# Gate projections of a decoder layer: hi and lo halves in one moving operand, a weight sum formed by accumulating DMAs, scratch reads moved a block ahead

## Chip, cores and metric

One core of a Trainium2 chip runs one launch. The metric is the time of the launch in microseconds, the median of several executions; the kernel before takes 1435.92 us.

## What is computed

A single layer: RMS norm with adaLN modulation, one input projection, a convolution branch and a differential-attention branch, both gated, merged by sigmoid gates of the input, and an output projection. The part that the change touches is the projection onto three of its column ranges, cz, m_conv ("mc") and m_attn ("ma"):

```python
h = rms_norm(x, g_pre[l]) * (1.0 + scale[:, None, :]) + shift[:, None, :]
p = h @ w_in[l]                                    # h: 512 x 2048
cv, cg, cz, q, k, v, az, m_conv, m_attn = jnp.split(p, offsets, axis=-1)
...
u = jax.nn.silu(u) * jax.nn.silu(cz)               # cz: 1024 columns
o = o.reshape(B, S, ATTN_WIDTH) * jax.nn.silu(az)
merged = jax.nn.sigmoid(m_conv) * y_conv + jax.nn.sigmoid(m_attn) * y_attn   # 2048 columns each
```

## The kernel before

Float32 operands are kept as sums of two float32r parts, hi and lo. `split` (L143) makes them: ScalarE copies hi (L145), VectorE subtracts for lo (L146). A product is then three matmuls, hi·hi, hi·lo and lo·hi, issued by `mm3` (L165, matmul on L167). h stands as 16 tiles of 128 rows (k = 0 to 15), each a pair tile `[128, 2, 512]` with hi and lo beside each other.

Stages in order: input norm and the conv projection, values, queries, keys and heads, then the az projection (L643 to L658) and then the gates (L803 to L824). The gates are 20 blocks of 256 output columns: 4 of cz, 8 of ma, 8 of mc. In a block `gemm_blocks` (L681) multiplies a 2 x 2 arrangement of weight blocks (a11, a21 in raw tile r1; a12, a22 in r2; each 128 x 8 x 128) with a 2 x 2 arrangement of h by Strassen's scheme in Winograd's form: seven products of 256 moving columns and eight k in place of eight products. It needs four sums of weights (s1 = a21 + a22, s2 = s1 + a11, s3 = a11 + a21, s4 = s2 + a12; L705, L706, L715, L724, on VectorE, 1024 elements wide) and sums of h (T1 to T4). Products go to three PSUM banks z, xx and y, in the order z, x, y, x, z, x, y; between them VectorE combines the results in 256-wide instructions (L711, L714, L718, L723, L727).

```python
def prod(ps, w, b, first):
    hi, lo = w
    for k in range(KH):
        mm3(ps[:, :H2], (hi[:, k, :], lo[:, k, :]), b[k], first and k == 0, k == KH - 1, not first, ordered)
    pump(rate[0])
```

The sums of h are made during the az stage by `block_sums` (L614), a generator whose steps `pump` (L478) inserts after each weight split there (three steps at a time); it splits T2 and T3 together (`t23`, 512 wide) and T4 for two k at a time. In the gates `pump` inserts steps of the convolution statistics (`conv_stats`, L747; `pmean` is its first matmul, behind the first product). `paced` and `ordered` keep the marked instructions in the order of the program; the rest is placed by a scheduler, and each engine runs its queue in order.

Temporaries come from the pool `mp`, which the stage before the gates holds under `front`; `front.close()` (L667) frees it and the gates open a pool of their own in the same memory. Weights come by `wraw` (L153, 1 MB each, three buffers, SP's queue) and are split by `wsplit` (L158) into hi and lo with three buffers each. Results are written to DRAM scratch by `spill` and read again by `fetch` (L433, L437), also on SP's queue. In ma, o and az are fetched after the block's products, multiplied (L820), split and spilled. GpSimd's queue has no DMA.

## Time and profile before

| | |
|---|---|
| runs | 1434.68, 1435.92, 1436.1 us; median 1435.92 |
| profiled execution | 1436.9 us, of it 1435.1 us span from the first to the last instruction |
| TensorE (PE) busy | 97% of the span |
| VectorE (DVE), ScalarE (ACT) busy | 75%, 36% |
| GpSimd (POOL) busy | 1.8 us |
| DMA queues | one of data, 237.31 MB |
| mean granted TensorE clock | 0.995 |

PE is matmuls, PEld weight loads, which overlap them; SPq is SyncE's queue of DMA issues. The start of an instruction and its duration are given, and durations of neighbours overlap in a pipeline, so the pace of an engine is the difference of starts. A wait is put down to what ended it. Stretches are given from the span's start.

### The profile page before, as it was taken

The page shows a single profiled execution, that of the slowest core. Times are in us where ns is not written, and L with a number is a line of the kernel's source. Part 1 is how long each engine was busy: PE and PEld are TensorE (multiplying, and loading weights), DVE is VectorE, ACT ScalarE, POOL GpSimd, SP SyncE. Part 2 cuts the span into 40 slices and gives each one's busy share as a digit, 9 for nine tenths or more (in the row PEclk, how much of TensorE's full clock was granted, in tenths as well). Part 3 has the DMA queues.
Part 4 walks back from the last instruction along what each step waited for, and adds up shares of the span by engine and source line. Part 5 has one row for each costly group of instructions (what it writes and reads, how often), then busy time and mean ns, then how long its engine had stood idle before and what let it go on. Part 6 is the DMA issues. An engine that isn't in the chain of part 4 may idle for free.

```text
span 1435.1 us, 20362 instructions
## 1 busy us (share of the span) xinstructions
PE 1397.3 (97%) x7999; PEld 1189.5 (83%) x7999; DVE 1080.9 (75%) x1750; ACT 522.1 (36%) x839; POOL 1.8 (0%) x8
## 2 busy tenths in 40 slices
PE   5899999999999999999999999999999999999997
PEld 4676787887777867788999999999998888888885
DVE  6997976988888887588988878777767676526645
...
GB/s 301 288 280 304 237 123 92 125 121 59 117 67 96 103 67 84 86 111 142 224 128 192 198 170 174 172 140 121 134 233 350 280 243 181 88 107 231 190 147 147
DMA packets 178338, 238.62 MB, mean 166 GB/s; under 512 B 8689, under 2 KB 119618, under 8 KB 177346
## 3 DMA queue, kind: packets, MB, share of 16 engines
q1 hardware_dynamic: 178242, 237.31, 49.9%
...
q14 instruction: 33, 0.27, 0.1%
HBM read 210.02 MB, written 27.26 MB: 165 GB/s over the span
## 4 chain that ended last, share of the span: by engine, by line
PE 90%; DVE 5%; DMA 2%; ACT 1%; issue 1%; SPq 0%; DVEq 0%; ACTq 0%
PE pw L167 12%; PE pc L167 11%; PE py_ya L167 6%; PE py_yc L167 6%; PE pv L167 6%; PE pg_az L167 5%; PE pg_q L167 5%; PE pg_k L167 5%; PE x_ma L167 5%; PE x_mc L167 4%; PE z_ma L167 3%; PE y_ma L167 3%; PE y_mc L167 3%; PE z_mc L167 3%; PE x_cz L167 2%; PE y_cz L167 2%
## 5 line engine op out<-in xcount | busy, mean ns | idle before, releaser
L500 DVE SCALAR_TENSOR_TENSOR cacc<-u,cw,cacc 128x511 f32<-128x511 f32 (+14 forms) x240 | 164.4, 728 | 0.0
L167 PE MATMUL pc<-hp,wh_c 128*128 128x512 f32 x512 | 159.9, 397 | 3.0 <-DVE part L369 1.2
L167 PE MATMUL pw<-wh_o,mgs 128*128 128x512 f32 x448 | 140.6, 393 | 0.0
L167 PEld LDWEIGHTS pc<-hp,wh_c 128*128 128x128 f32 x512 | 95.6, 190 | 29.0 <-issue 2.7
L167 PE MATMUL pc<-hp,wl_c 128*128 128x512 f32 x256 | 99.0, 396 | 2.1 <-DVE wl_c L146 2.1
L167 PEld LDWEIGHTS pw<-wh_o,mgs 128*128 128x128 f32 x448 | 84.1, 188 | 18.9 <-ACT fsq L932 0.7
L167 PE MATMUL pw<-wl_o,mgs 128*128 128x512 f32 x224 | 87.2, 389 | 0.0
L369 DVE TENSOR_TENSOR part<-pc,part 128x512 f32<-128x512 f32 x96 | 64.7, 687 | 25.3 <-PE pc L167 25.0
L167 PE MATMUL pv<-wh_v,hp 128*128 128x512 f32 x256 | 82.8, 397 | 0.9 <-DVE part L369 0.9
L167 PE MATMUL pg_q<-hp,wh_q 128*128 128x512 f32 x256 | 82.7, 398 | 0.0
L167 PE MATMUL pg_az<-hp,wh_az 128*128 128x512 f32 x256 | 81.5, 395 | 0.0
L167 PE MATMUL pg_k<-hp,wh_k 128*128 128x512 f32 x256 | 80.1, 392 | 0.0
L167 PE MATMUL py_ya<-ya,wh_ya 128*128 128x512 f32 x256 | 78.7, 389 | 0.0
L146 DVE TENSOR_TENSOR wl_o<-wr_o,wh_o 128x1024 fp32r<-128x1024 f32 x28 | 34.2, 1222 | 52.7 <-ACT wh_o L145 52.7
L145 ACT CAST wh_c<-wr_c 128x1024 fp32r<-128x1024 f32 (+1 forms) x36 | 34.2, 955 | 104.0 <-DMA wr_c<-in_w_in_dram 54.9
L889 DVE SCALAR_TENSOR_TENSOR accg<-adag,cact,accg 128x512 f32<-128x512 f32 x60 | 45.1, 751 | 32.2 <-DMA adag<-in_w_ada_dram 31.1
L145 ACT CAST wh_o<-wr_o 128x1024 fp32r<-128x1024 f32 x28 | 29.5, 1052 | 104.5 <-PE pw L167 93.0
L167 PEld LDWEIGHTS pc<-hp,wl_c 128*128 128x128 f32 x256 | 48.5, 190 | 14.1 <-DVE wl_c L146 3.3
L167 PEld LDWEIGHTS pv<-wh_v,hp 128*128 128x128 f32 x256 | 47.8, 188 | 14.3 <-issue 4.5
L167 PEld LDWEIGHTS pg_az<-hp,wh_az 128*128 128x128 f32 x256 | 47.7, 188 | 12.0 <-issue 2.7
L167 PEld LDWEIGHTS pg_q<-hp,wh_q 128*128 128x128 f32 x256 | 47.2, 188 | 12.4 <-issue 2.8
L167 PEld LDWEIGHTS py_ya<-ya,wh_ya 128*128 128x128 f32 x256 | 48.0, 188 | 9.9
...
## 6 DMA issues: line engine op xcount, KB each, us to landing
ada<-in_w_ada_dram SPq DMA_DIRECT2D x128, 256.0 KB, 5.4
wr_ma<-in_w_in_dram SPq DMA_DIRECT2D x16, 1024.0 KB
wr_mc<-in_w_in_dram SPq DMA_DIRECT2D x16, 1024.0 KB, 5.2
...
wr_o<-in_w_o_dram SPq DMA_DIRECT2D x16, 1024.0 KB, 5.1
...
wr_v<-in_w_in_dram SPq DMA_DIRECT2D x8, 1024.0 KB, 5.1
wr_q<-in_w_in_dram SPq DMA_DIRECT2D x8, 1024.0 KB, 5.0
```

The source lines that it names most:

```text
L145: nc.scalar.copy(hi, src)
L146: i = nc.vector.tensor_tensor(lo, src, hi.bitcast(F32), op=ALU.subtract)
L167: mm = nc.tensor.matmul(ps, a[p], b[q], start=start and i == 0, stop=stop and i == 2, skip_group_check=more)
L369: nc.vector.tensor_tensor(part[i], ps[f], part[i], op=ALU.add)
L500: paced(nc.vector.scalar_tensor_tensor(cvo[t][:, s:], u[t][:, :S - s], wj, cvo[t][:, s:], op0=ALU.mult, op1=ALU.add))
L889: nc.vector.scalar_tensor_tensor(acc, raw[:, k, :], s1, acc, op0=ALU.mult, op1=ALU.add)
```

## The change

`prod` takes hi and lo of h (or of T1 to T4) as one moving operand of 2 x 256 columns: a matmul of 512 columns writes hi·hi into the lower half of the bank and hi·lo into the upper, and a second of 256 columns adds lo·hi to the lower. All z and y products do so; x products do so in mc alone. Each result is then read in two pieces, so further 256-wide instructions appear on VectorE and a copy on ScalarE. For this T2, T3 and T4 are split one k at a time into `[hi | lo]` tiles by `halves_of`.

s1 is no longer a VectorE sum: GpSimd's queue loads a21 into a tile and a second DMA adds a22 to it. In mc, s3 is formed likewise, by a DMA that adds a11 onto a21 in r1. `block_load` issues the loads of a block while the block before it runs, r2 behind the fourth product. `pump` runs after every second product. o and az are fetched at the head of the ma block and split in place; the gates' pool has 10 temporaries in place of 12.

```diff
@@ -31,7 +31,7 @@
...
-NTEMP2 = 12
+NTEMP2 = 10
...
@@ -333,8 +333,8 @@
                 k = kb + b
                 hf = page(f"hf_{k}")
                 nc.scalar.activation(hf, xn[k], AF.Identity, scale=scl[:, b:b + 1], bias=sh[:, b:b + 1])
-                g = pair_of(f"hp_{k}")
-                h[k] = hi, lo = g[:, 0, :], g[:, 1, :]
+                hp[k] = pair_of(f"hp_{k}")
+                h[k] = hi, lo = hp[k][:, 0, :], hp[k][:, 1, :]
                 split(hf, hi, lo)
             yield
...
@@ -608,8 +608,14 @@
-    T23, T4 = [None] * KH, [None] * KH
+    T2, T3, T4 = [None] * KH, [None] * KH, [None] * KH
     t1s = [temp(f"t1_{i}") for i in range(KH // 2)]
+    def halves_of(src, name):
+        g = page(name, F32R)
+        split(src, g[:, :H2], g[:, H2:], pace=True)
...
             paced(nc.vector.tensor_tensor(t23[:, :H2], f2[:, H2:], t1, op=ALU.add))
             paced(nc.vector.tensor_tensor(t4[:, half], f2[:, :H2], t23[:, :H2], op=ALU.subtract))
-            hi, lo = page(f"t23h_{k}", F32R), page(f"t23l_{k}", F32R)
-            split(t23, hi, lo, pace=True)
-            T23[k] = (hi, lo)
+            T2[k] = halves_of(t23[:, :H2], f"t2_{k}")
+            T3[k] = halves_of(t23[:, H2:], f"t3_{k}")
             yield
-            if k % 2:
-                hi, lo = page(f"t4h_{k}", F32R), page(f"t4l_{k}", F32R)
-                split(t4, hi, lo, pace=True)
-                for i in range(2):
-                    T4[k - 1 + i] = (hi[:, i * H2:(i + 1) * H2], lo[:, i * H2:(i + 1) * H2])
-                yield
+            T4[k] = halves_of(t4[:, half], f"t4_{k}")
+            yield
-    B11 = [(hi[:, :H2], lo[:, :H2]) for hi, lo in h[:KH]]
-    T1 = [(hi[:, H2:], lo[:, H2:]) for hi, lo in h[:KH]]
-    T2 = [(hi[:, :H2], lo[:, :H2]) for hi, lo in T23]
-    T3 = [(hi[:, H2:], lo[:, H2:]) for hi, lo in T23]
-    B21 = [(hi[:, :H2], lo[:, :H2]) for hi, lo in h[KH:]]
-    B22 = [(hi[:, H2:], lo[:, H2:]) for hi, lo in h[KH:]]
+    B11 = [g[:, :, :H2] for g in hp[:KH]]
+    T1 = [g[:, :, H2:] for g in hp[:KH]]
+    B21 = [g[:, :, :H2] for g in hp[KH:]]
+    B22 = [g[:, :, H2:] for g in hp[KH:]]
+    blocks, done = {}, [0]
+    def block_load(src, c0, name):
+        s1 = mp.tile([P, KH, P], F32, tag="s1", bufs=2, name=f"s1_{name}")
+        v = src.rearrange("(t p) n -> p t n", p=P)
+        nc.gpsimd.dma_start(out=s1, in_=v[:, :KH, c0 + P:c0 + 2 * P])
+        nc.gpsimd.dma_start(out=s1, in_=v[:, KH:, c0 + P:c0 + 2 * P], accum_op=ALU.add)
         r1 = wraw(src, 0, KH, c0, 256, f"{name}_1")
-        r2 = wraw(src, KH, KH, c0, 256, f"{name}_2")
-        a11, a21 = r1[:, :, :P], r1[:, :, P:]
+        if name[:2] == "mc":
+            nc.gpsimd.dma_start(out=r1[:, :, P:], in_=v[:, :KH, c0:c0 + P], accum_op=ALU.add)
+        blocks[name] = [s1, r1]
+        yield
+        blocks[name].append(wraw(src, KH, KH, c0, 256, f"{name}_2"))
+    def gemm_blocks(name):
+        s1, r1, r2 = blocks.pop(name)
+        a11, s3 = r1[:, :, :P], r1[:, :, P:]
         a12, a22 = r2[:, :, :P], r2[:, :, P:]
-        def tsum(i):
-            return mp.tile([P, KH, P], F32, tag="ws", bufs=2, name=f"ws_{name}_{i}")
-        def prod(ps, w, b, first):
+        s2 = mp.tile([P, KH, P], F32, tag="s2", bufs=1, name=f"s2_{name}")
+        xwide = name[:2] == "mc"
+        def prod(ps, w, b, first, wide=True):
             hi, lo = w
+            psv = ps.rearrange("p (a n) -> p a n", a=2)
             for k in range(KH):
-                mm3(ps[:, :H2], (hi[:, k, :], lo[:, k, :]), b[k], first and k == 0, k == KH - 1, not first, ordered)
-            pump(rate[0])
+                if wide:
+                    ordered(nc.tensor.matmul(psv, hi[:, k, :], b[k], start=first and k == 0, stop=False,
+                                             skip_group_check=True))
+                    ordered(nc.tensor.matmul(ps[:, :H2], lo[:, k, :], b[k][:, 0, :], start=False, stop=k == KH - 1,
+                                             skip_group_check=True))
+                else:
+                    mm3(ps[:, :H2], (hi[:, k, :], lo[:, k, :]), (b[k][:, 0, :], b[k][:, 1, :]), first and k == 0,
+                        k == KH - 1, not first, ordered)
+            done[0] += 1
+            if done[0] % 2:
+                pump(rate[0])
+        def comb(out, ps, a, op0, op1, wide=True):
+            nc.vector.tensor_tensor(out, ps[:, :H2], a, op=op0)
+            if wide:
...
+                nc.vector.tensor_tensor(out, ps[:, H2:], out, op=op1)
         z, xx, y = [gbank(f"{n}_{name}", tag) for n, tag in (("z", "g"), ("x", "s"), ("y", "g"))]
-        s1, s2 = tsum(1), tsum(2)
         ta, tb = temp(f"ta_{name}"), temp(f"tb_{name}")
-        q1, u2 = ta[:, :H2], ta[:, H2:]
+        q1, u2 = tb[:, :H2], ta[:, H2:]
         w11 = wsplit(a11, f"{name}_a11")
-        nc.vector.tensor_tensor(s1, a21, a22, op=ALU.add)
+        prod(z, w11, B11, True)
         nc.vector.tensor_tensor(s2, s1, a11, op=ALU.add)
-        prod(z, w11, B11, True)
         nc.scalar.copy(q1, z[:, :H2])
+        nc.vector.tensor_tensor(q1, z[:, H2:], q1, op=ALU.add)
         ws2 = wsplit(s2, f"{name}_s2")
-        prod(xx, ws2, T2, True)
+        prod(xx, ws2, T2, True, xwide)
         nc.vector.tensor_tensor(u2, q1, xx[:, :H2], op=ALU.subtract)
+        if xwide:
+            nc.vector.tensor_tensor(u2, u2, xx[:, H2:], op=ALU.subtract)
...
         ws1 = wsplit(s1, f"{name}_s1")
         prod(y, ws1, T1, True)
-        nc.vector.tensor_tensor(tb[:, H2:], q1, y[:, :H2], op=ALU.add)
-        nc.vector.tensor_tensor(a21, a11, a21, op=ALU.add)
-        ws3 = wsplit(a21, f"{name}_s3")
-        prod(xx, ws3, T3, False)
-        nc.vector.tensor_tensor(tb[:, H2:], xx[:, :H2], tb[:, H2:], op=ALU.subtract)
+        comb(tb[:, H2:], y, q1, ALU.add, ALU.add)
+        if name[:2] != "mc":
+            nc.vector.tensor_tensor(s3, a11, s3, op=ALU.add)
+        ws3 = wsplit(s3, f"{name}_s3")
+        prod(xx, ws3, T3, False, xwide)
+        next(loads[0], None)
+        comb(tb[:, H2:], xx, tb[:, H2:], ALU.subtract, ALU.add, xwide)
         w12 = wsplit(a12, f"{name}_a12")
         prod(z, w12, B21, False)
+        nc.scalar.copy(ta[:, :H2], z[:, :H2])
+        nc.vector.tensor_tensor(ta[:, :H2], z[:, H2:], ta[:, :H2], op=ALU.add)
         w22 = wsplit(a22, f"{name}_a22")
-        prod(xx, w22, T4, False)
-        nc.vector.tensor_tensor(tb[:, :H2], xx[:, :H2], q1, op=ALU.subtract)
+        prod(xx, w22, T4, False, xwide)
+        comb(q1, xx, q1, ALU.subtract, ALU.add, xwide)
         nc.vector.tensor_tensor(s2, s2, a12, op=ALU.add)
         ws4 = wsplit(s2, f"{name}_s4")
         prod(y, ws4, B22, False)
-        nc.vector.tensor_tensor(u2, u2, y[:, :H2], op=ALU.add)
-        return z, ta, tb
-    def silu2(i, z, ta, tb):
+        comb(u2, y, u2, ALU.add, ALU.add)
+        return ta, tb
...
+    todo = [(C_CZ + j * 256, f"cz{j}") for j in range(4)]
+    todo += [(c0 + j * 256, f"{name}{j}") for c0, name in ((C_MA, "ma"), (C_MC, "mc")) for j in range(8)]
+    todo = deque(todo)
+    loads = [block_load(w_in[0], *todo.popleft())]
+    for _ in range(2):
+        next(loads[0], None)
+    def next_load():
+        loads[0] = block_load(w_in[0], *todo.popleft()) if todo else iter(())
+        next(loads[0], None)
     for pair in range(4):
-        gs = silu2(pair, *gemm_blocks(w_in[0], C_CZ + pair * 256, f"cz{pair}"))
+        next_load()
+        gs = silu2(pair, *gemm_blocks(f"cz{pair}"))
         for f in range(2):
             spill(f"cz{2 * pair + f}", gs[f])
     for c0, name in ((C_MA, "ma"), (C_MC, "mc")):
         for j in range(8):
-            z, ta, tb = gemm_blocks(w_in[0], c0 + j * 256, f"{name}{j}")
+            next_load()
+            if name == "ma":
+                o, az = temp(f"o_{j}"), temp(f"az_{j}")
+                fetch(f"o{j}", o)
+                fetch(f"az{j}", az)
+            ta, tb = gemm_blocks(f"{name}{j}")
             g0, g1 = temp(f"{name}0_{j}"), temp(f"{name}1_{j}")
-            nc.scalar.activation(g0[:, :H2], z[:, :H2], AF.Tanh, scale=0.5)
-            nc.scalar.activation(g0[:, H2:], ta[:, H2:], AF.Tanh, scale=0.5)
+            nc.scalar.activation(g0, ta, AF.Tanh, scale=0.5)
             nc.scalar.activation(g1, tb, AF.Tanh, scale=0.5)
             spill(f"{name}{2 * j}", g0)
             spill(f"{name}{2 * j + 1}", g1)
             if name == "ma":
-                o, az = temp(f"o_{j}"), temp(f"az_{j}")
-                fetch(f"o{j}", o)
-                fetch(f"az{j}", az)
                 nc.vector.tensor_tensor(o, o, az, op=ALU.mult)
-                hi, lo = temp(f"oh_{j}", F32R), temp(f"ol_{j}", F32R)
-                split(o, hi, lo)
-                spill(f"yah{j}", hi.bitcast(F32))
-                spill(f"yal{j}", lo.bitcast(F32))
+                split(o, az.bitcast(F32R), o.bitcast(F32R))
+                spill(f"yah{j}", az)
+                spill(f"yal{j}", o)
```

In the rows below, names are the program's with buffer numbers; `s_cz` is s1 or s2 of block cz0, `t_7` the pieces of T2, T3, T4 for k = 7, `wh`/`wl` hi and lo of weights.

On PE, the first product (z) of the first gates block; before:

```order
L167 MATMUL z_cz_5616<-hp_515,wh_cz_a_5623 128x256 x2
L167 MATMUL z_cz_5616<-hp_515,wl_cz_a_5624 128x256
L167 MATMUL z_cz_5616<-hp_723,wh_cz_a_5623 128x256 x2
L167 MATMUL z_cz_5616<-hp_723,wl_cz_a_5624 128x256
L167 MATMUL z_cz_5616<-hp_728,wh_cz_a_5623 128x256 x2
```

and now:

```order
L713 MATMUL z_cz_5649<-hp_515,wh_cz_a_5654 128x512
L715 MATMUL z_cz_5649<-hp_515,wl_cz_a_5655 128x256
L713 MATMUL z_cz_5649<-hp_723,wh_cz_a_5654 128x512
L715 MATMUL z_cz_5649<-hp_723,wl_cz_a_5655 128x256
L713 MATMUL z_cz_5649<-hp_728,wh_cz_a_5654 128x512
```

Two of the three matmuls of a k have become one of twice the columns.

On DVE, from the end of the az stage into the first gates block; before, t4l is the last split of a sum of h and sz the last results of az:

```order
L146 TENSOR_TENSOR t4l_5523<-t_6_5443,t4h_5522 128x512 [waits Activation_49]
L146 TENSOR_TENSOR wl_az_12_5551<-wr_az_8_5510,wh_az_12_5550 128x1024
L146 TENSOR_TENSOR wl_cz_a_5624<-wr_cz_1_5612,wh_cz_a_5623 128x1024 [waits DMAHW5_49,PE_49]
L705 TENSOR_TENSOR ws_cz_1_5619<-wr_cz_1_5612,wr_cz_2_5614 128x1024 [waits DMAHW6_49,DMAHW7_49,DMAHW0_49,DVE_49]
L706 TENSOR_TENSOR ws_cz_2_5620<-ws_cz_1_5619,wr_cz_1_5612 128x1024 [waits DVE_49]
L715 TENSOR_TENSOR wr_cz_1_5612<-wr_cz_1_5612 128x8x128
L146 TENSOR_TENSOR wl_cz_s_5657<-ws_cz_2_5620,wh_cz_s_5656 128x1024 [waits PE_49,Activation_49]
L724 TENSOR_TENSOR ws_cz_2_5620<-ws_cz_2_5620,wr_cz_2_5614 128x1024 [waits DVE_49]
L657 SCALAR_TENSOR_TENSOR sz_5594<-sz_5594,pg_az_0_5427 128x512 [waits Activation_49]
```

and now:

```order
L146 TENSOR_TENSOR t_7_5572<-hf_7_5533,t_7_5572 128x256 [waits Activation_49]
L146 TENSOR_TENSOR t_7_5575<-t_6_5489,t_7_5575 128x256 [waits Activation_49]
L748 TENSOR_TENSOR wr_cz_1_5646<-wr_cz_1_5646 128x8x128 [waits DMAHW1_49]
L658 SCALAR_TENSOR_TENSOR sz_5618<-sz_5618,pg_az_0_5432 128x512 [waits Activation_49]
L658 SCALAR_TENSOR_TENSOR sz_5623<-sz_5623,pg_az_1_5433 128x512 [waits Activation_49]
L737 TENSOR_TENSOR tb_cz_5653<-z_cz_5649,tb_cz_5653 128x256 [waits DMAHW7_49,DMAHW6_49,Activation_49]
L735 TENSOR_TENSOR s_cz_5648<-s_cz_5636,wr_cz_1_5639 128x1024 [waits DMASW2_49]
L146 TENSOR_TENSOR wl_cz_s_5680<-s_cz_5648,wh_cz_s_5679 128x1024 [waits Activation_49]
```

The sum s2 (L706 before, L735 now) stood ahead of the last az results; it now stands behind them and behind the addition to z's copy (L737), and waits for a DMA of GpSimd's queue.

On POOL, the first DMAs of its queue (before there are none):

```order
L687 DMA s_cz_5636<-in_w_in_dram 128x8x128 [waits DMAHW3_49,DMAHW4_49,DMAHW2_49,DMAHW5_49,DMAHW1_49,DMAHW6_49,DMAHW0_49,DMAHW7_49,DVE_49,PE_49]
L687 DMA s_cz_5643<-in_w_in_dram 128x8x128
L688 DMA s_cz_5636<-in_w_in_dram 128x8x128 [waits DMASW0_49]
L688 DMA s_cz_5643<-in_w_in_dram 128x8x128 [waits DMASW1_49]
L687 DMA s_cz_5846<-in_w_in_dram 128x8x128 [waits DMASW2_49,DVE_49]
L688 DMA s_cz_5846<-in_w_in_dram 128x8x128 [waits DMASW4_49]
```

The first waits for the users of the memory that the az stage held (its DVE wait is for `t_7_5575<-t_6_5489`, the last split of k = 7); each accumulating DMA (L688) waits for the load (L687) that it adds to.

## Rows read from the trace of the kernel before

**Rows 1.** The page, part 1: busy time, share of the span, instructions.

```profile
PE 1397.3 (97%) x7999; PEld 1189.5 (83%) x7999; DVE 1080.9 (75%) x1750; ACT 522.1 (36%) x839; POOL 1.8 (0%) x8
```

**Rows 2.** Stretches in cz, ma, mc: us, busy (x instructions) by engine, PEclk, DMA share, GB/s.

```profile
705.30:725.60 20.30, 20.30 (x171) 20.30 (x171) 19.44 (x27) 10.58 (x14) 0.00 (x0) 1.00 0.59 195
847.40:867.70 20.30, 20.30 (x171) 20.30 (x170) 16.26 (x18) 9.49 (x13) 0.00 (x0) 1.00 0.56 182
948.90:969.20 20.30, 20.30 (x171) 20.30 (x171) 15.19 (x17) 8.97 (x12) 0.00 (x0) 1.00 0.39 130
```

**Rows 3.** Waits of PE over the span: us in total, times, longest.

```profile
PE x_mc L167 <- DVE tb_mc L718: 1.1, 1, 1.1
```

**Rows 4.** Timeline of PE in ma: start us, us, engine line op, count.

```profile
819.82 0.28 PE L167 MATMUL x_ma<-t23h,wh_ma_s 128*128 128x256 f32 x1
...
820.54 0.40 PE L167 MATMUL z_ma<-hp,wh_ma_a 128*128 128x256 f32 x2
```

**Rows 5.** Timeline of PE in the stage after the gates.

```profile
1101.72 0.61 PE L167 MATMUL py_ya<-ya,wh_ya 128*128 128x512 f32 x2
...
1105.12 0.61 PE L167 MATMUL py_ya<-ya,wh_ya 128*128 128x512 f32 x2
```

**Rows 6.** DVE's groups in the gates: count, busy us, mean ns, idle before.

```profile
L705 DVE TENSOR_TENSOR ws_mc<-wr_mc,wr_mc 128x1024 f32<-128x1024 f32 x8 | 9.8, 1220 | 3.5 <-DMA wr_mc<-in_w_in_dram 3.5
```

**Rows 7.** Timeline of DVE before the gates.

```profile
643.08 0.69 DVE L657 SCALAR_TENSOR_TENSOR sz<-sz,pg_az 128x512 f32<-128x512 f32 x1 [1.21 <-ACT sz L656]
...
645.13 0.69 DVE L621 TENSOR_TENSOR hf<-hp 128x512 f32<-128x512 f32 x1
645.73 0.42 DVE L627 TENSOR_TENSOR t<-hf 128x256 f32<-128x256 f32 x1
646.07 0.42 DVE L146 TENSOR_TENSOR hp<-t,hp 128x256 fp32r<-128x256 f32 x1
...
657.78 1.22 DVE L146 TENSOR_TENSOR wl_cz_a<-wr_cz,wh_cz_a 128x1024 fp32r<-128x1024 f32 x1
658.92 1.22 DVE L705 TENSOR_TENSOR ws_cz<-wr_cz,wr_cz 128x1024 f32<-128x1024 f32 x1
```

**Rows 8.** Timeline of PE at the entry of the gates.

```profile
648.37 0.62 PE L167 MATMUL pg_az<-hp,wh_az 128*128 128x512 f32 x2
...
664.69 0.40 PE L167 MATMUL z_cz<-hp,wh_cz_a 128*128 128x256 f32 x2
...
668.02 0.68 PE L167 MATMUL x_cz<-t23h,wh_cz_s 128*128 128x256 f32 x1
```

**Rows 9.** Timeline of ACT at the entry.

```profile
661.56 1.06 ACT L145 CAST wh_cz_s<-ws_cz 128x1024 fp32r<-128x1024 f32 x1 [5.55 <-issue]
...
668.59 0.37 ACT L708 COPY ta_cz<-z_cz 128x256 f32<-128x256 f32 x1
```

**Rows 10.** DMA: packets of 16 to 20 us; issues in the gates; longest piece of the chain.

```profile
DMA packets 2339, 1.16 MB, mean 290 GB/s; under 512 B 73, under 2 KB 2339, under 8 KB 2339
...
wr_mc<-in_w_in_dram SPq DMA_DIRECT2D x16, 1024.0 KB, 5.2
...
scratch_ma<-ma SPq DMA_DIRECT2D x16, 256.0 KB, 2.0
...
915.17 8.62 DMA wr_mc<-in_w_in_dram
```

**Rows 11.** Stretches at the end of the run, columns as rows 2.

```profile
1424.00:1425.00 1.00, 0.74 (x4) 0.27 (x2) 1.00 (x3) 0.23 (x1) 0.00 (x0) 1.00 0.79 311
...
1429.00:1430.00 1.00, 0.00 (x0) 0.00 (x0) 1.00 (x2) 0.00 (x0) 0.00 (x0) 0.50 0.39 164
```

**Rows 12.** After one-column matmuls: timeline of PE, then stretches.

```profile
141.02 0.77 PE L167 MATMUL pc<-hp,wl_c 128*128 128x512 f32 x1
...
144.00:145.00 1.00, 1.00 (x3) 0.72 (x3) 0.61 (x1) 1.00 (x3) 0.00 (x0) 0.50 0.22 41
...
146.00:147.00 1.00, 1.00 (x6) 0.79 (x6) 0.75 (x2) 1.00 (x2) 0.00 (x0) 1.00 0.77 254
```

More of the change, by code (lines that the diff above doesn't have):

```diff
@@ L171, in mm3 @@
         return mm
-    h = [None] * KT
+    h, hp = [None] * KT, [None] * KT
     part = [None] * 16
@@ L610, in hybrid_trunk @@
     KH = KT // 2
-    T23, T4 = [None] * KH, [None] * KH
+    T2, T3, T4 = [None] * KH, [None] * KH, [None] * KH
     t1s = [temp(f"t1_{i}") for i in range(KH // 2)]
+    def halves_of(src, name):
+        g = page(name, F32R)
+        split(src, g[:, :H2], g[:, H2:], pace=True)
+        return g.rearrange("p (a n) -> p a n", a=2)
     def block_sums():
@@ L679, in ordered @@
         tc.stamp_issue_order_token(instruction.ins, "gates")
-    def gemm_blocks(src, c0, name):
-        r1 = wraw(src, 0, KH, c0, 256, f"{name}_1")
-        r2 = wraw(src, KH, KH, c0, 256, f"{name}_2")
-        a11, a21 = r1[:, :, :P], r1[:, :, P:]
+    blocks, done = {}, [0]
[4 more added lines that the diff above has]
+        nc.gpsimd.dma_start(out=s1, in_=v[:, KH:, c0 + P:c0 + 2 * P], accum_op=ALU.add)
+        r1 = wraw(src, 0, KH, c0, 256, f"{name}_1")
+        if name[:2] == "mc":
[3 more added lines that the diff above has]
+        blocks[name].append(wraw(src, KH, KH, c0, 256, f"{name}_2"))
@@ L726, in gemm_blocks, with silu2 @@
         prod(y, ws4, B22, False)
-        nc.vector.tensor_tensor(u2, u2, y[:, :H2], op=ALU.add)
-        return z, ta, tb
-    def silu2(i, z, ta, tb):
+        comb(u2, y, u2, ALU.add, ALU.add)
+        return ta, tb
+    def silu2(i, ta, tb):
         g0, g1 = temp(f"g0_{i}"), temp(f"g1_{i}")
-        nc.scalar.activation(g0[:, :H2], z[:, :H2], AF.Tanh, scale=0.5)
-        nc.scalar.activation(g0[:, H2:], ta[:, H2:], AF.Tanh, scale=0.5)
-        nc.scalar.activation(g1, tb, AF.Tanh, scale=0.5)
-        nc.vector.scalar_tensor_tensor(g0[:, :H2], g0[:, :H2], 1.0, z[:, :H2], op0=ALU.add, op1=ALU.mult)
-        nc.vector.scalar_tensor_tensor(g0[:, H2:], g0[:, H2:], 1.0, ta[:, H2:], op0=ALU.add, op1=ALU.mult)
-        nc.vector.scalar_tensor_tensor(g1, g1, 1.0, tb, op0=ALU.add, op1=ALU.mult)
+        for g, t in ((g0, ta), (g1, tb)):
+            nc.scalar.activation(g, t, AF.Tanh, scale=0.5)
+            nc.vector.scalar_tensor_tensor(g, g, 1.0, t, op0=ALU.add, op1=ALU.mult)
         return g0, g1
@@ L808, in hybrid_trunk @@
         for j in range(8):
-            z, ta, tb = gemm_blocks(w_in[0], c0 + j * 256, f"{name}{j}")
+            next_load()
[4 more added lines that the diff above has]
+            ta, tb = gemm_blocks(f"{name}{j}")
             g0, g1 = temp(f"{name}0_{j}"), temp(f"{name}1_{j}")
-            nc.scalar.activation(g0[:, :H2], z[:, :H2], AF.Tanh, scale=0.5)
-            nc.scalar.activation(g0[:, H2:], ta[:, H2:], AF.Tanh, scale=0.5)
+            nc.scalar.activation(g0, ta, AF.Tanh, scale=0.5)
             nc.scalar.activation(g1, tb, AF.Tanh, scale=0.5)
@@ L881, in gate @@
         for k0 in range(0, KT, 2):
-            raw = mp.tile([P, 2, S], F32, tag="ws", bufs=2, name=f"adag_{n}_{k0}")
+            raw = mp.tile([P, 2, S], F32, tag="s1", bufs=2, name=f"adag_{n}_{k0}")
             nc.sync.dma_start(out=raw, in_=ada_v[:, k0:k0 + 2, 2 * D + n * 512:2 * D + (n + 1) * 512])
```

## Prediction

> **What bounds the kernel now.** I read the page first. PE is busy 97% of the span [rows 1]: the kernel is as fast as TensorE gets through its instructions, and another engine counts only where it makes PE wait. Then the three kinds of gates blocks in stretches of 20.3 us, about one block each [rows 2]: PE is busy throughout at full granted clock, DVE 19.4 us in the cz stretch (it also does the convolution statistics), 16.3 in ma and 15.2 in mc, and DMA has a share of 0.59, 0.56 and 0.39. The waits of PE name one inside the gates that is worth a term: 1.1 us behind L718 [rows 3], where VectorE stood for a weight load in the first mc block [rows 6]; that load's 8.62 us is the longest DMA piece of the whole chain [rows 10].
>
> So what the change is worth is how densely PE issues, less any new wait. The density is a difference of starts, since busy times overlap. In a product of 256 columns six matmuls take 820.54 - 819.82 = 0.72 us, 0.120 each [rows 4]; 512 columns wide, fifteen take 1105.12 - 1101.72 = 3.40 us, 0.2267 each [rows 5]. 512 columns cost 0.2267 and not 2 x 0.120 = 0.240: each matmul with its weight load carries 0.0133 us that doesn't grow with its columns.
>
> **Merged matmuls.** Per tile k two matmuls of 0.120 become one of 0.2267: 0.0133 us less. A block has seven products of eight k; z and y (four) are merged everywhere, x (three) in mc alone: 12 blocks x 32 + 8 blocks x 56 = 832 pairs, so 832 x 0.0133 = **-11.1 us**, all of it on PE's path. Its bounds: 0, if a 512-column write over two pieces took as long as the two it replaces, and 22, if the hidden weight load saved as much again; I take 11.1, since the row it is nearest to is a 512-column accumulation of the same types.
>
> The rule in the Trainium skill that speaks against this is in "TensorE: Matmul & The Clock Gate", section "Back-to-back issue gap": an isolated matmul takes N/2.4 ns + 2.5 at the fast clock, so merging would save 832 x 2.5 ns = 2.1 us, and the whole sum below would come out near +7 instead of -2. The trace disagrees for loads paired with matmuls: 13.3 ns per instruction, twice measured [rows 4, 5].
>
> **VectorE and ScalarE, steady blocks.** Off DVE go the first weight sum, 1.22 us a block, and in mc a second [rows 6]. On it come the additions of the upper half: four per block in cz and ma, seven in mc, 0.42 us each, as other 256-wide ones [rows 7]. That is 4 x 0.42 - 1.22 = +0.5 us in cz and ma and 7 x 0.42 - 2.44 = +0.5 in mc, against a block that is 0.4 (32 x 0.0133) or 0.7 us shorter. DVE stays under PE by over 3 us in ma and mc; in cz the pump now runs after every second product, so the statistics spread over twice the blocks. ScalarE gains one copy of 0.37 us [rows 9] a block at 9 to 10.6 us of 20.3. I cost all this at nothing; the cover is the spare DVE time, and a weight split is begun up to two products (5.6 us) before PE needs it. The new second reading of x in mc delays the next x product only if it comes later than y's 2.8 us.
>
> **GpSimd's queue and DMA, steady blocks.** Each block adds two DMAs of 0.5 MB in 512-byte pieces, in mc a third: 48 in all, on a queue that carried none. Such pieces moved at 290 GB/s when they filled the engines [rows 10]: 1.8 us each. If the accumulating one moves twice the bytes (it reads its destination as well), a block of ma has 5.4 us more in 20.3, a share of 0.56 + 0.27 = 0.83, and one of mc 0.39 + 0.45 = 0.84. Below 1, and s1 is loaded when its buffer of two blocks before comes free, over 25 us ahead. The second half of the raw weights is issued after the fourth product, about 8 us before the block's end, against 5.2 us to land [rows 10]. o and az, fetched a block ahead, move in front of the spills on SP's queue, and no wait of PE names them. Cost: nothing. With the sum gone that stood for the load, the 1.1 us of [rows 3] goes too: **-1.1 us**.
>
> **The az stage before the gates.** The smaller splits and two weight sums now stand between its weight splits. From 643.08 VectorE has no pause [rows 7]. Counting the changed order from there, 0.60 us per 512-wide, 0.34 per 256-wide and 1.14 per 1024-wide instruction (differences of starts in [rows 7]), the last pair's second weight split ends at 649.5, where PE wants it 0.9 us after 648.37 [rows 8]: **+0.3 us** with the hand-over. The last of the three splits of k = 7 ends at about 662.4: 8 of 0.60, 29 of 0.34 and 4 of 1.14 us make 19.2.
>
> **The entry of the gates.** This is the new wait. s1's buffer lies where the stage before had its temporaries, so the first load on GpSimd waits for that last split, 662.4. Before, DVE had both sums of cz0 done when the cast of the second began at 661.56 [rows 9], and PE went from z (664.69) through a mean of the statistics to x at 668.02 [rows 8]. Now: issue 0.4; load 2.0 + 1.8 = 3.8 (2.0 is what a 256 KB store needs to land, 1.8 the bytes at 290 GB/s); issue 0.4; accumulate 2.0 + 3.6 = 5.6. Landed at 662.4 + 10.2 = 672.6. Then s2's sum, 1.22, its cast, 1.06 [rows 9], 0.2 of hand-overs: x begins at 675.1 in place of 668.0, 7.1 us. The third matmul needs the low half, 1.2 us behind the high one with 0.24 us of work between: 0.9 more. **+8.0 us.** On DVE s2's sum also stands behind the addition for z (z's end 664.69 + 2.8 = 667.5, copy 0.37, addition 0.42), so the wait is at least 2.9 + 0.9 = 3.8 us even if the DMAs cost nothing; if each took the 8.62 us of the longest piece, it is 15. I stay near the middle, since those two rows are the same tensor's loads alone and under a crowd.
>
> For a plain 0.5 MB load the Trainium skill ("DMA: Bandwidth & Descriptors", section "Anatomy of one DMA — SWDGE (gpsimd) path") gives 2.0 us + bytes/436 GB/s, 3.2 us. Two of those would land s1 at 669.6, and the wait would be 5.0; no row shows a DMA on this queue.
>
> After seven idle microseconds the clock counts. At the end of the run PE stops at 1424.7, and by 1429 the granted clock reads 0.50 [rows 11]; after the stretch of one-column matmuls dense work from 141.02 still ran at 0.50 in 144 to 145 and at 1.00 in 146 to 147 [rows 12], about 4.2 us at 1.2 in place of 2.4 GHz, which loses half: **+2.1 us**.
>
> **Sum:** -11.1 - 1.1 + 0.3 + 8.0 + 2.1 = -1.8 us. The profiled execution took 1436.9 us, the median is 1435.92, 1.0 lower; from the median: **1434.2 us**.
>
> **Rivals.** (a) The entry is short. If both DMAs take 3.2 us and PE's pause of 4.1 us leaves the clock at full, the sum is -11.1 - 1.1 + 0.3 + 5.0 = -6.9: 1429.0. For it: DMA's share is but 0.59 in a cz block [rows 2]. Against it: that share is another load's, and two DMAs stand in series.
> (b) Slower: the accumulate is slow. With 8.62 us for each DMA, the entry costs 15 + 0.9 and the sum is -11.1 - 1.1 + 0.3 + 15.9 + 2.1 = +6.1: 1442.0. It decides against the change from a chain of 14.9 us on (10.2 + 4.7). For it: a piece of 8.62 did happen, and the queue is untried. Against it: the share of 0.59, as under (a).
> (c) The merge saves nothing (the matmul over two pieces takes 0.240 us): -1.1 + 0.3 + 10.1 = +9.3, 1445.2. Against it: [rows 5].
>
> **How the numbers follow.** Forecast 0.42, (a) 0.33, (b) 0.20, (c) 0.05. 0.2% is 2.9 us, about what a measurement of this kernel can tell from no change. The forecast reaches from -5 to +2 by its unknown DMA times: 0.13 of it faster, 0.25 the same, 0.04 slower. (a) is faster; (b) is slower but for 0.02; (c) is slower. Faster 0.46, same 0.27, slower 0.27. The range 1427 to 1442 holds the forecast, (a) and most of (b); the likeliest case alone spans 1431 to 1438.
>
> **What would show it.** Right: in a merged product starts 0.2267 and 0.120 apart; a pause of PE before x_cz of the first block of about 7 us, ended by ScalarE's cast behind DVE's s2 behind a DMA on GpSimd's queue; a granted clock of 0.50 for some microseconds after it; no other wait of PE above 1 us in the gates; the stage after the gates about 2 us earlier than before. Wrong: waits that come back in every block, with DMA's share near 1; a pause under 4 us or over 12; or merged starts 0.240 apart.

## The result: 38 us slower, and the profile after

The changed kernel takes 1473.76 us (median of 4), the kernel before 1435.3 beside it: a ratio of 1.0279, 95% interval 1.0249 to 1.031. The prediction, 1434.2 with a range from 1427 to 1442, was wrong. (The kernel before ran beside each group of runs; its medians below are 1435.3, 1435.88, 1435.11 and 1436.18, so times of different groups compare to about 1 us.)

The page of the profile after: busy time and instructions (part 1), and its two queues of data (part 3: packets, MB, share of 16 engines' span; q1 is SP's, q0 is GpSimd's). [rows 1] has the first line before.

```profile
PE 1399.8 (95%) x7167; PEld 1146.8 (78%) x7167; DVE 1086.9 (74%) x1834; ACT 525.5 (36%) x851; POOL 63.6 (4%) x56
...
q1 hardware_dynamic: 178242, 237.31, 48.2%
q0 software_dynamic: 32000, 25.17, 10.9%
```

PE has 832 matmuls fewer and the same busy time: it waits more, 95% of a longer span. The longest waits of PE in the gates and behind them (us in total, times, longest), where the kernel before had one of 1.1 us, [rows 3]:

```profile
PE x_cz L167 <- ACT wh_cz_s L145: 8.2, 1, 8.2
...
PE x_ma L167 <- DVE ta_ma L741: 4.4, 4, 1.8
PE py_ya L167 <- ACT wh_ya L145: 3.2, 1, 3.2
PE x_ma L167 <- DVE wl_ma_s L146: 3.0, 3, 1.4
PE x_ma L167 <- DVE tb_ma L726: 2.7, 1, 2.7
PE x_cz L167 <- DVE wl_cz_s L146: 2.5, 3, 1.3
```

Stretch by stretch, from the starts of the first products in PE's timeline (profiled executions, us):

| stretch | before | after | difference |
|---|---|---|---|
| up to the gates | 664.7 | 662.2 | -2.5 |
| block cz0 | 21.0 | 32.7 | +11.7 |
| blocks cz1 to ma7 (11) | 224.1 | 248.8 | +24.7 |
| blocks of mc (8) | 162.6 | 158.9 | -3.7 |
| after the gates | 362.7 | 368.4 | +5.7 |

The first row is the execution's own: over the profiled executions of all kernels here the gates began between 662.2 and 666.3. The other four make 38.4 us.

**The entry** went as forecast in its chain. POOL's timeline there (start, us, engine line op, count, idle time before and what ended it):

```profile
660.14 1.97 POOL L687 DMA_DIRECT2D s_cz<-in_w_in_dram  x2 [657.24 <-DVE t L146]
665.58 1.58 POOL L688 DMA_DIRECT2D s_cz<-in_w_in_dram  x1 [3.46 <-DMA s_cz<-in_w_in_dram]
```

DVE's timeline, its last split of the stage before and s2's sum:

```profile
659.08 0.42 DVE L146 TENSOR_TENSOR t<-t,t 128x256 fp32r<-128x256 f32 x1
...
671.97 1.23 DVE L735 TENSOR_TENSOR s_cz<-s_cz,wr_cz 128x1024 f32<-128x1024 f32 x1 [5.88 <-DMA s_cz<-in_w_in_dram]
```

PE's timeline:

```profile
665.05 1.02 PE L783 MATMUL pmean<-csum,ones 128*128 128x512 f32 x2
674.32 0.80 PE L167 MATMUL x_cz<-t,wh_cz_s 128*128 128x256 f32 x2 [8.25 <-ACT wh_cz_s L145]
675.58 0.58 PE L167 MATMUL x_cz<-t,wl_cz_s 128*128 128x256 f32 x1 [0.46 <-DVE wl_cz_s L146]
675.96 0.63 PE L167 MATMUL x_cz<-t,wh_cz_s 128*128 128x256 f32 x2
...
676.61 0.63 PE L167 MATMUL x_cz<-t,wh_cz_s 128*128 128x256 f32 x2
```

And a stretch behind it, columns as [rows 2]:

```profile
676.00:680.00 4.00, 4.00 (x20) 4.00 (x20) 2.94 (x3) 0.17 (x1) 0.92 (x1) 0.50 0.33 58
```

VectorE's last split ended at 659.5, POOL's loads followed at 660.14, the accumulating DMA at 665.58, s2's sum at 671.97. x began at 674.32, 9.27 us behind `pmean` where it was 0.46. A k (three matmuls) then took 676.61 - 675.96 = 0.65 us in place of 0.36 while the granted clock stood at 0.50, the lower of its two levels (1.2 in place of 2.4 GHz); it did so until about 680.9.

**Blocks cz1 to ma7** hold what the prediction had not seen. DVE's waits in the gates, two of them:

```profile
DVE wr_ma L748 <- DMA wr_ma<-in_w_in_dram: 23.5, 8, 4.8
DVE o L868 <- DMA az<-scratch_az: 12.0, 5, 5.3
```

L748 is s3's sum of a cz or ma block; it waited 23.5 us in all, 8 times, for the load of its weights (two more such waits, in cz blocks, are 4.4 us). PE's own waits in these eleven blocks add up to about 22 us. One of the waits of L748, in block ma1, in DVE's timeline:

```profile
782.66 1.22 DVE L146 TENSOR_TENSOR wl_ma_s<-s_ma,wh_ma_s 128x1024 fp32r<-128x1024 f32 x1
788.69 1.23 DVE L748 TENSOR_TENSOR wr_ma<-wr_ma 128x1024 f32<-128x1024 f32 x1 [4.81 <-DMA wr_ma<-in_w_in_dram]
...
790.16 1.22 DVE L146 TENSOR_TENSOR wl_ma_s<-s_ma,wh_ma_s 128x1024 fp32r<-128x1024 f32 x1
```

The load, in the timeline of SP's queue:

```profile
778.53 0.50 SPq L155 DMA_DIRECT2D wr_ma<-in_w_in_dram  x1
```

And PE's timeline, the first two matmuls of ma1's first y product:

```profile
788.69 0.40 PE L713 MATMUL y_ma<-hp,wh_ma_s 128*128 128x512 f32 x1
791.43 0.39 PE L715 MATMUL y_ma<-hp,wl_ma_s 128*128 128x256 f32 x1 [2.35 <-DVE wl_ma_s L146]
```

The load was issued at 778.53. DVE turned to the sum at 788.69 - 4.81 = 783.88 and stood until the load had landed, 10.2 us after its issue. Behind it stood the split of s1, which PE needs for y: y began at 788.69 with the high half, and PE then stood 2.35 us for the low half. The order on DVE, from the program, says whose sum it is (in brackets the semaphores; DMAHW is that of a load on SP's queue):

```
L146 TENSOR_TENSOR wl_ma1_s2_6756<-s2_ma1_6726,wh_ma1_s2_6755 128x1024 [waits Activation_49]
L748 TENSOR_TENSOR wr_ma2_1_6720<-wr_ma2_1_6720 128x8x128 [waits DMAHW0_49]
L726 TENSOR_TENSOR ta_ma0_6504<-y_ma0_6503,ta_ma0_6504 128x256 [waits PE_49]
L146 TENSOR_TENSOR wl_ma1_s1_6786<-s1_ma1_6491,wh_ma1_s1_6785 128x1024 [waits Activation_49]
```

It is the *next* block's, ma2's: it stands a block ahead of its need, right behind its load. Before, the sum of ma2 stood in the middle of ma1, behind its s1, and waited for VectorE itself alone:

```
L705 TENSOR_TENSOR ws_ma2_1_7115<-wr_ma2_1_7108,wr_ma2_2_7110 128x1024 [waits DMAHW7_49,DMAHW5_49]
L718 TENSOR_TENSOR tb_ma1_6879<-x_ma1_6874,tb_ma1_6879 128x256 [waits DVE_49,PE_49]
L715 TENSOR_TENSOR wr_ma2_1_7108<-wr_ma2_1_7108 128x8x128 [waits DVE_49]
```

The code gives a reason: s3 is written over a21. Before, the VectorE sum s1 had to read a21 first, and it needs r2 as well, which SP's queue loaded 14 us later (760.10 and 774.05). With s1 taken from DRAM nothing holds s3 back but its own load.

The other wait, of the product of o and az, has to do with the fetch of az. The code asks for it at the head of the block, but in ma1 to ma7 SP issued it 4 to 10 us behind the block's start, while the product had moved from behind the block's end into the block. In ma7, which began at 920.8 (the timelines of SP's queue and of DVE):

```profile
925.17 0.89 SPq L438 DMA_DIRECT2D az<-scratch_az  x1
934.22 0.69 DVE L868 TENSOR_TENSOR o<-o,az 128x512 f32<-128x512 f32 x1 [5.26 <-DMA az<-scratch_az]
```

The blocks of mc show that busy DMA engines alone don't stop PE. There s3 is no sum on VectorE, and no o and az are fetched. Blocks cz1 to ma7 and then mc, columns as [rows 2]:

```profile
694.90:943.70 248.80, 227.03 (x1515) 206.30 (x1514) 190.81 (x268) 107.51 (x138) 28.59 (x23) 0.99 0.78 217
943.70:1102.60 158.90, 158.90 (x898) 136.95 (x897) 124.17 (x168) 71.52 (x88) 25.61 (x19) 1.00 0.90 220
```

PE was busy throughout mc at a DMA share of 0.90, and waited about 22 us before, at 0.78.

The loads were slower too. Landing in the gates and behind (issues: KB, median us), where [rows 10] has 5.2 us for a load of this size; the second row is loads and accumulating DMAs together:

```profile
wr_ma<-in_w_in_dram SPq DMA_DIRECT2D x16, 1024.0 KB, 7.5
...
s_ma<-in_w_in_dram POOLq DMA_DIRECT2D x16, 512.0 KB, 6.4
```

**The merged products** ran at two paces. The second z of mc0 and of mc3, each with the start of the next product (PE's timeline):

```profile
955.15 0.40 PE L713 MATMUL z_mc<-hp,wh_mc_a 128*128 128x512 f32 x1
...
957.98 0.40 PE L713 MATMUL x_mc<-t,wh_mc_a 128*128 128x512 f32 x1
...
1014.93 0.39 PE L713 MATMUL z_mc<-hp,wh_mc_a 128*128 128x512 f32 x1
...
1017.70 0.39 PE L713 MATMUL x_mc<-t,wh_mc_a 128*128 128x512 f32 x1
```

957.98 - 955.15 = 2.83 us for most products, 1017.70 - 1014.93 = 2.77 for ten in mc, against 2.88 unmerged. The third and fourth product of most mc blocks took longer, 2.91 and 2.89 us.

**The stage after the gates.** PE's 3.2 us there (`py_ya`) are for the second weight load of that stage. Before, it was issued 14.8 us ahead of the stage's start (row under merge_alone); now 5.2 us behind it (1102.6), in the timeline of SP's queue:

```profile
1107.79 0.38 SPq L155 DMA_DIRECT2D wr_ya<-in_w_attn_out_dram  x1
```

Behind the wait the granted clock read 0.51 from 1117.8 to 1121.2, by estimate another 1.7 us.

### The profile page after: what moved, and what is told of

Its sections match the earlier page's. It is cut to its first block, busy times and chain, and to the rows that moved or that the text cites. A ratio compares the mean times of both kernels' runs of the same rounds, so it can differ in the third digit from the quotient of the medians.

```text
span 1471.0 us, 18915 instructions
## 1 busy us (share of the span) xinstructions
PE 1399.8 (95%) x7167; PEld 1146.8 (78%) x7167; DVE 1086.9 (74%) x1834; ACT 525.5 (36%) x851; POOL 63.6 (4%) x56
## 3 DMA queue, kind: packets, MB, share of 16 engines
q1 hardware_dynamic: 178242, 237.31, 48.2%
q0 software_dynamic: 32000, 25.17, 10.9%
```

## Experiments

Theory O (order): VectorE's instructions that wait for a load stand too early, in front of splits that PE needs. Theory C (traffic): GpSimd's DMAs make loads late whatever the order. The first column is the median, the stretches (us) are from the profiled execution of each; the kernel before has 21.0, 224.1, 162.6 and 362.7, the changed kernel 32.7, 248.8, 158.9 and 368.4:

| run | us | ratio to before (95%) | cz0 | cz1 to ma7 | mc | after |
|---|---|---|---|---|---|---|
| s3_held | 1459.14 | 1.0156 (1.0139 to 1.0172) | 32.7 | 233.8 | 158.9 | 369.0 |
| s3_dma | 1467.08 | 1.0206 (1.0182 to 1.023) | 33.9 | 240.4 | 158.3 | 369.3 |
| entry_vec | 1459.72 | 1.0165 (1.0145 to 1.0185) | 20.8 | 247.1 | 158.6 | 369.0 |
| merge_alone | 1444.28 | 1.0054 (1.0039 to 1.0069) | 20.8 | 229.5 | 160.3 | 369.1 |
| small_acc | 1454.17 | 1.0137 (1.0122 to 1.0152) | 28.3 | 231.8 | 159.0 | 368.1 |
| held2_entry | 1440.6 | 1.0038 (1.0024 to 1.0052) | 20.8 | 226.0 | 158.3 | 368.0 |
| held2_entry_ya | 1433.31 | 0.9984 (0.9971 to 0.9998) | 20.8 | 224.6 | 158.3 | 362.7 |
| held2_entry_ya_pairs | 1428.37 | 0.9958 (0.9944 to 0.9973) | 20.6 | 222.2 | 156.1 | 363.0 |
| best_eights | 1427.57 | 0.9942 (0.9927 to 0.9957) | 20.6 | 223.3 | 156.4 | 362.8 |
| merge_ya_pairs | 1434.6 | 0.9995 (0.9985 to 1.0005) | 20.6 | 225.1 | 159.0 | 362.9 |
| best_xnarrow | 1431.73 | 0.9966 (0.9953 to 0.9979) | 20.6 | 224.6 | 158.3 | 363.1 |

### s3_held: s3's sum behind its own block's split of s1

```diff
-        ws1 = wsplit(s1, f"{name}_s1")
+        ws1 = wsplit(s1, f"{name}_s1", True)
...
-            nc.vector.tensor_tensor(s3, a11, s3, op=ALU.add)
+            paced(nc.vector.tensor_tensor(s3, a11, s3, op=ALU.add))
```

> Changed kernel, but the VectorE sum s3 of a cz or ma block is kept behind the block's own s1 weight split instead of a block ahead. Theory O (order): the stalls of blocks cz1 to ma7, about 27 us, come from s3's sum standing in VectorE's queue right behind the load of its weights, a block before it is needed; held back, nearly all of them go: 1446 to 1453 us (the entry of the gates, about 12 us, stays). Theory C (traffic): GpSimd's DMAs make every weight load late, whatever reads it first, so the stalls move to the next reader: 1465 us or more.

14.6 us less than the changed kernel, between the two forecasts; cz1 to ma7 lost 15.0 of 24.7. No wait of DVE for r1 in L748 is left. What remains sits in ma1, ma4 and ma7, and DVE's waits name the next instruction of the same kind, the product of o and az that waits for its fetch:

```profile
DVE o L868 <- DMA az<-scratch_az: 12.9, 7, 4.1
```

So theory O holds for the larger part. It missed its range (1446 to 1453) because it had counted one instruction where there were two.

### s3_dma: s3 by an accumulating DMA everywhere

```diff
-        if name[:2] == "mc":
+        if True:
             nc.gpsimd.dma_start(out=r1[:, :, P:], in_=v[:, :KH, c0:c0 + P], accum_op=ALU.add)
...
-        if name[:2] != "mc":
-            nc.vector.tensor_tensor(s3, a11, s3, op=ALU.add)
```

> Changed kernel, but s3 is formed by an accumulating DMA in all 20 blocks, not in mc alone: 12 more accumulating DMAs, no VectorE instruction that waits for them a block ahead. Theory O: the stalls of cz1 to ma7 go, 1446 to 1455 us. Theory C: more traffic on the same engines in the blocks that already stall, 1474 us or more.

6.7 us less, outside both forecasts: the sum's stalls are gone and others have come, since the traffic grew. Queue q0's share from 700 to 1060 us (MB, share; 38.0% in the changed kernel) and the landing of r1 and r2 (7.5 there):

```profile
q0 software_dynamic: 37874, 26.78, 49.5%
...
wr_ma<-in_w_in_dram SPq DMA_DIRECT2D x16, 1024.0 KB, 8.5
```

The product of o and az then waited 20.7 us on DVE, in 7 waits. Traffic isn't free; it acts through whichever VectorE instruction waits for a transfer.

### small_acc: the same order, less traffic

```diff
-        nc.gpsimd.dma_start(out=s1, in_=v[:, KH:, c0 + P:c0 + 2 * P], accum_op=ALU.add)
+        nc.gpsimd.dma_start(out=s1[:, :1, :], in_=v[:, KH:KH + 1, c0 + P:c0 + 2 * P], accum_op=ALU.add)
```

The kernel leaves out seven of the eight slices of a22 in s1. The order on every engine is that of the changed kernel but for one exchange on DVE in cz0 (L735 and L737).

> Changed kernel, in which the DMA that accumulates into s1 moves one of its eight k slices; seven eighths of the second addend of s1 are left out. The order of all instructions stays. If the traffic of the accumulating DMAs alone makes the stalls of cz1 to ma7 (theory C), nearly all 27 us go with it, and 2 to 3 us of the entry: 1444 us or less. If the stalls come from s3's sum standing right behind a load that has just been issued (theory O), a load takes about 5 us even alone, and half of them stay: 1455 to 1465 us.

0.8 us under theory O's range, 10 above C's. DVE's wait for r1 in ma fell from 23.5 us to (DVE's waits)

```profile
DVE wr_ma L748 <- DMA wr_ma<-in_w_in_dram: 8.2, 6, 2.3
```

and cz1 to ma7 by 17.0 us. A wait was 1.4 us in the mean in place of 2.9. Order and traffic work together: the order decides that VectorE stands in front of the load, the traffic for how long. Either one taken away gives back 60 to 70% of the 24.7 us.

### entry_vec: s1 and s2 of block cz0 on VectorE

```diff
+        if name == "cz0":
+            nc.vector.tensor_tensor(s1, s3, a22, op=ALU.add)
+            nc.vector.tensor_tensor(s2, s1, a11, op=ALU.add)
```

(and neither DMA for that block).

> Changed kernel, but s1 of the first block alone is summed on VectorE from the raw weights, and its s2 directly behind. The entry stall is that of the chain load, accumulate, s2, cast: PE's wait of 8.3 us before the first x product goes, and with it the 2 to 3 us at half clock: 1462 to 1466 us, 8 to 12 below the changed kernel. Rival: VectorE is itself late there (it still splits the sums of h until about 660 us), then 3 us or less is gained.

14.0 us less by the medians, more than the 8 to 12 expected (the medians carry some noise: the changed kernel's runs lie between 1472.6 and 1479.1); in its trace cz0 takes 20.8 us, 11.9 less, and x follows `pmean` by 0.46 us again. The entry stall is the chain of the two DMAs.

### merge_alone: the merged matmuls without any DMA sum

The loads, sums, `pump` and fetches of the kernel before, with `prod`, `comb` and `halves_of` of the change:

```diff
-        nc.gpsimd.dma_start(out=s1, in_=v[:, :KH, c0 + P:c0 + 2 * P])
-        nc.gpsimd.dma_start(out=s1, in_=v[:, KH:, c0 + P:c0 + 2 * P], accum_op=ALU.add)
...
+        nc.vector.tensor_tensor(s1, s3, a22, op=ALU.add)
+        nc.vector.tensor_tensor(s2, s1, a11, op=ALU.add)
...
-            if done[0] % 2:
-                pump(rate[0])
+            pump(rate[0])
```

> The kernel before with the wide matmuls and the split of T2, T3, T4 into [hi | lo] alone: sums s1 and s3 on VectorE, loads, pump, o and az as before, no DMA on GpSimd's queue. Theories O and C both expect the gain that the merged matmuls show in the trace, 0.05 us a merged product (96 + 40 of them less the later second reading in mc, about 4.4 us) and the mc wait of 1.1: 1429 to 1432 us. Rival M: the extra VectorE additions eat it, 1435 us or more.

8.4 us slower than before: both theories missed, and rival M is part of the answer. (The merged products are 48 + 56, not 96 + 40.) cz1 to ma7 cost 5.4 more: PE waits for VectorE in cz2, where the statistics run and the block takes 24.8 us for 20.2, and every second ma block is 0.6 to 0.9 longer than the one beside it. Another 6.4 us lie after the gates, as in the changed kernel: PE waits there for the second weight load of that stage. In the timeline of SP's queue it was issued at

```profile
1080.14 0.38 SPq L155 DMA_DIRECT2D wr_ya<-in_w_attn_out_dram  x1
```

5.6 us after the stage began (1074.51). In the kernel before, it was issued at

```profile
1057.64 0.38 SPq L155 DMA_DIRECT2D wr_ya<-in_w_attn_out_dram  x1
```

14.8 us ahead of its stage (1072.45). Between the stage's first weight load and this one two spills stood on SP's queue before, and now 29 fetches and spills, though the buffer waits for the same split of the last mc block; why the scheduler put it there was not found.

### held2_entry, held2_entry_ya: the order held, then the load

Both have the edit of entry_vec as well.

```diff
+        ws1 = wsplit(s1, f"{name}_s1", True)
+        if not xwide:
+            paced(nc.vector.tensor_tensor(s3, a11, s3, op=ALU.add))
+        paced(nc.vector.tensor_tensor(u2, q1, xx[:, :H2], op=ALU.subtract))
...
+        ws3 = wsplit(s3, f"{name}_s3", True)
...
+        ws4 = wsplit(s2, f"{name}_s4", True)
...
+                paced(nc.vector.tensor_tensor(o, o, az, op=ALU.mult))
```

> Changed kernel with the first block's s1 and s2 on VectorE, and with VectorE's order held in a cz or ma block: s1 split, s3, then the first reading of x, then s3's split, and the product o times az behind the split of s4. Theory O, extended to the product o times az that waits for its fetch: s3_held's rest (about 10 us in blocks ma1, ma4 and ma7) goes as well, 1436 to 1441 us with the entry. Rival: the waits only move to the next reader, 1445 us or more.

As theory O had it: 1440.6, and cz1 to ma7 at 226.0. What PE still waits for longest in the gates, and the wait behind them (us in total, times, longest):

```profile
PE py_ya L167 <- ACT wh_ya L145: 3.3, 1, 3.3
PE x_ma L167 <- DVE wl_ma_s L146: 1.3, 3, 0.6
PE x_ma L167 <- DVE ta_ma L749: 1.1, 1, 1.1
```

```diff
+        with tc.high_priority(offset=400) if name == "ya1" else nullcontext():
+            raw = wraw(src, 0, 8, c0, 256, name)
```

> As held2_entry, with the second weight load of the stage after the gates given priority, so that it is issued about 14 us earlier on SyncE's queue. PE's wait of 3.2 us there and the half clock behind it, together 5 to 6 us, go: 1431 to 1436 us, 4 to 6 below held2_entry. Rival: the load is early, but the DMA engines are full there, and another load is late instead: 2 us or less.

7.3 us less, of which the trace shows 5.3 after the gates; and the wait for `wh_ya` is gone from PE's list, which now begins:

```profile
PE x_ma L167 <- DVE wl_ma_s L146: 1.3, 3, 0.6
```

### held2_entry_ya_pairs, best_eights: the pace of a merged product

Both add to held2_entry_ya.

```diff
+                    if k % 2:
+                        continue
+                    for j in (k, k + 1):
+                        ordered(nc.tensor.matmul(psv, hi[:, j, :], b[j], start=first and j == 0, stop=False,
+                                                 skip_group_check=True))
+                    for j in (k, k + 1):
+                        ordered(nc.tensor.matmul(ps[:, :H2], lo[:, j, :], b[j][:, 0, :], start=False,
+                                                 stop=j == KH - 1, skip_group_check=True))
```

> As held2_entry_ya, with the merged product issued as two wide matmuls (k, k + 1) and then their two narrow ones. In the changed kernel a merged product takes 2.83 us in most blocks and 2.77 in some; if the slower pace comes from a change of width at every matmul, it becomes 2.77 everywhere: 104 products by 0.06, 5 to 6 us less than held2_entry_ya. Rival: the pace has another cause, no difference beyond 1 us.

4.9 us less: 1428.37, 6.7 under the kernel before. In PE's timeline four matmuls, two wide and two narrow, now take 960.96 - 960.27 = 0.69 us, and every merged product that PE doesn't wait in 2.787:

```profile
960.27 0.63 PE L717 MATMUL x_mc<-t,wh_mc_a 128*128 128x512 f32 x2
...
960.96 0.62 PE L717 MATMUL x_mc<-t,wh_mc_a 128*128 128x512 f32 x2
```

```diff
-                    for j in (k, k + 1):
+                for j in range(KH):
```

(both loops over all eight k, for held2_entry_ya_pairs)

> As held2_entry_ya_pairs, with all eight wide matmuls of a merged product ahead of its eight narrow ones: one change of width in a product where the pairs have eight and the changed kernel sixteen. If each change of width costs, a product goes from 2.785 to about 2.77 us: 104 by 0.015, and the low half of the weights is needed later: 1425.5 to 1428 us. Rival: one matmul behind another of its own width is all that counts and the pairs have got it: 1428 to 1429 us.

1427.57, no difference that the runs can tell. In PE's timeline a product takes 965.29 - 962.49 = 2.80 us, no less than with pairs (2.793 over all, against 2.787):

```profile
962.49 2.00 PE L714 MATMUL y_mc<-hp,wh_mc_s 128*128 128x512 f32 x8
...
965.29 2.00 PE L714 MATMUL z_mc<-hp,wh_mc_a 128*128 128x512 f32 x8
```

A cost for every change of width, as I had it, would have made this the fastest; that theory falls. What makes the alternating order slower in most products stays open.

### merge_ya_pairs, best_xnarrow: which parts pay

merge_ya_pairs is merge_alone with the edits of held2_entry_ya and held2_entry_ya_pairs:

```diff
+        with tc.high_priority(offset=400) if name == "ya1" else nullcontext():
...
+                    for j in (k, k + 1):
```

> merge_alone (s1 and s3 on VectorE, no DMA on GpSimd's queue) with the early weight load of the next stage and with the pairs. From its 1444.3: 5 to 6 for the load, 4.7 for the pairs: 1433 to 1436 us, so that 5 us or more of what held2_entry_ya_pairs gains on the kernel before would be due to VectorE's freed time. Rival: VectorE isn't short and the DMA sums are not needed: 1428 to 1430 us.

1434.6, as before the change. Of the 6.2 us between it and held2_entry_ya_pairs 5.8 lie in cz1 to mc of the traces (2.9 and 2.9). PE's waits there are 6.2 us, 4.8 of them behind VectorE, in cz2, in every second ma block and in mc, where 1.8 had been left. So the DMA sums pay through VectorE's freed time, in the main.

```diff
-        xwide = name[:2] == "mc"
+        xwide = False
```

> As held2_entry_ya_pairs, with the x products of mc in 256-wide matmuls again: 24 products of 2.88 in place of 2.785 us, 2.3 us slower: 1430 to 1431.5 us. Rival: the second reading of x delays as much as the wide product gains, no difference beyond 1 us.

1431.73, 3.4 us more by the medians, of different groups (the ratios to the kernel before, 0.9966 and 0.9958, overlap in their intervals). The trace is clearer: mc takes 158.3 - 156.1 = 2.2 us more, as 24 x 0.093 = 2.2 says. So once the readings of x keep their place, the wide x pays in mc.

## Why the prediction was wrong

| term | predicted | in the traces |
|---|---|---|
| merged matmuls | -11.1 | 104 products x (2.83 - 2.88) = -5.2; with pairs 104 x (2.787 - 2.88) = -9.7 |
| wait in mc0 | -1.1 | -1.1 (gone) |
| az stage | +0.3 | +0.6 |
| entry, with the clock | +10.1 | 11.7 + 4 x 0.05 = +11.9 |
| steady blocks | 0 | cz1 to ma7: 24.7 + 44 x 0.05 = +26.9 |
| stage after the gates | not in the sum | +5.7 |

The right column, at the pace of 2.83, makes 38.8; the medians differ by 38.5. (In the left one 1435.92 - 1.8 is 1434.1, not 1434.2, which changes nothing.)

**The step that failed** is the pair of parts "VectorE and ScalarE, steady blocks" and "GpSimd's queue and DMA, steady blocks", both of which ended in "nothing". I costed VectorE by busy time against the block, with "over 3 us" to spare, and the DMA engines by a share below 1. Both were about right: DVE's busy time grew by 6 us in the whole run, and the share, forecast at 0.83 in ma and 0.84 in mc, was 0.78 and 0.90. But a share says nothing of an engine that runs its queue in order: it stood still for 23.5 us in front of a load while the work behind was due. s3's sum I didn't mention: in cz and ma it stayed, and I had not asked what held it in its place. The order on DVE that stands ahead of the prediction has the sign: its line L748 sums `wr_cz_1_5646`, the weights of cz1 (those of cz0 are `wr_cz_1_5639`), a block early and behind its own load alone. "o and az, fetched a block ahead" failed as well: az came 4 to 10 us into its own block, and the product stood in front of due work. The share also hid that a load lands in 7.5 us, and in the case of ma1 in 10.2, where I took 5.2. s3_held and small_acc show both halves, held2_entry the product of o and az with them.

**No rival had it.** (a) and (b) turned on the entry and (c) on the merge; the slowest, (c), ended at 1445.2 with a chance of 0.05. The condition that would have shown it was in the text, "waits that come back in every block, with DMA's share near 1", but had been given neither a price nor a chance.

**The entry was right in its chain**, and nearly in its size: PE's waits were 8.25 + 0.46 = 8.7 us for 8.0, and the rest of the 11.9, about 3 us for 2.1, went with the lower clock, at which PE worked from 674.3 to about 680.9. That the times themselves fit so well (s2's sum at 671.97 where the DMAs were to land at 672.6, x at 674.32 for 675.1) is luck in part: VectorE's last split ended at 659.5 and not at 662.4, 2.5 us of it because this execution reached the gates earlier, and the two DMAs took 671.97 - 659.50 = 12.5 us for 10.2. entry_vec took the stall away with one edit. The estimate of 3.2 us for such a load by the Trainium skill ("DMA: Bandwidth & Descriptors", section "Anatomy of one DMA — SWDGE (gpsimd) path") was too short here: from the load's issue at 660.14 to that of the accumulating DMA behind it at 665.58 is 5.4 us, with the load of the next block issued in between.

**The merged matmuls** gain in the way forecast, and half as much at the pace in which they run. The saving of 0.0133 us a pair, which I had from one difference of two uniform streams, is reached nearly (9.7 of 11.1) when equal widths stand side by side, not when they alternate. The estimate of 2.1 us by the Trainium skill ("TensorE: Matmul & The Clock Gate", section "Back-to-back issue gap") is less than either; the section gives that formula for an isolated matmul, and says that in a stream of weight loads and matmuls, such as this one, both set the spacing. So it did not speak against the forecast.

**The stage after the gates** was left out of the sum altogether; the prediction has it only as beginning about 2 us earlier. Its loads share SP's queue with the gates, and one of them came 20 us later against the stage's start (5.2 us behind it, for 14.8 ahead).
